# Layer-1 windowed attention: masks added on VectorE in the pass that takes a head's maximum, scores of the edge blocks as 512-column products

## The chip, the cores and the metric

The kernel runs on one core of one Trainium2 chip. The metric is the device time of one execution in microseconds; the time of a kernel is the median of its runs. TensorE (PE; its weight loads are shown apart as PEld) multiplies, VectorE (DVE) and ScalarE (ACT) work on what it leaves in PSUM, GpSimd (POOL) and the DMA queues work on SBUF only.

## What is computed

The reference is a trunk of two layers over 512 latent tokens with 256 context tokens in front. Layer 0 mixes with an mLSTM, layer 1 with windowed attention, and each layer ends in a squared-ReLU MLP. The change touches the attention of layer 1, cut here to what matters:

```python
# 16 query heads in 4 groups, one key/value head per group, head size 64, blocks of 128 queries
def block(args):                         # one of 4 query blocks
    j, qb = args
    kb = lax.dynamic_slice_in_dim(kp, j * SWA_BLOCK, 3 * SWA_BLOCK, axis=1)   # previous, own, next key block
    valid = (jnp.abs(rel) <= WINDOW) & (kpos >= 0) & (kpos < n_tok)           # WINDOW = 128
    s_lat = jnp.einsum("bqhgd,bkhd->bhgqk", qb, kb).astype(F32) * scale
    s_lat = jnp.where(valid, s_lat, -jnp.inf)
    s_ctx = jnp.einsum("bqhgd,bchd->bhgqc", qb, ck).astype(F32) * scale       # 256 context keys, no mask
    m = jnp.maximum(jnp.maximum(jnp.max(s_lat, -1), jnp.max(s_ctx, -1)), sink_g)
    p_lat, p_ctx = jnp.exp(s_lat - m[..., None]), jnp.exp(s_ctx - m[..., None])
    den = jnp.sum(p_lat, -1) + jnp.sum(p_ctx, -1) + jnp.exp(sink_g - m)
    o = jnp.einsum("bhgqk,bkhd->bqhgd", p_lat, vb) + jnp.einsum("bhgqc,bchd->bqhgd", p_ctx, cv)
    return o / jnp.moveaxis(den, 3, 1)[..., None]
```

A middle query block (j = 1, 2) sees three key blocks and the context, 640 keys; its previous block needs a triangular mask and its next block the opposite one. An edge block (j = 0, 3) sees two key blocks and the context, 512 keys, and needs one of the masks.

## The kernel before

**Scores** (`scores`, lines 1903 to 1958) makes the scores of one group g and one block j, head by head; it is a generator that yields after each of the four heads. Queries `qs` are the stationary operand, 128 tokens of one head with the high and low halves of the float split stacked, and the keys `ks` (two versions, `k0` and `k1`) are moved past them, so that each score is the sum of two products. A head of a middle block fills 640 columns of a PSUM tile `s` of its own; two heads of an edge block share one tile of 1024 columns, 512 each (`per = 2`). A tile is two PSUM banks, and the pool `sc` holds two tiles. For each head TensorE does, in order:

- L1925, L1926: two products of 256 columns against the context keys (`cx`),
- L1927: a product of 384 or 256 columns against the keys of the window (`lat`),
- L1929 and L1931: the masks. A mask `msk` of 128 × 128 in bf16, with 0 or a large negative number, is added to the first and to the last 128 columns of `lat` by a product with the identity `idb`; an edge block has only one of the two,
- L1932: the second product of the window.

Then VectorE takes the maximum of the tile (L1938 `mx`, for both heads of an edge pair at once), and makes from it and the sink the negative bias `nb` (L1940). ScalarE takes the exponential from PSUM into `e` and sums it into `den` (L1945). After every second head come the sink's exponential `es` (L1950, L1952), the denominator (L1953, L1954), and on GpSimd the division of `e` (L1956).

**Weigh** (`weigh`, from line 1960) turns the four heads' `e` by transposes on TensorE (L1972, into a tile `pt`), copies them by ScalarE to `ph` (L1977), and multiplies them with the values (L1989, L1995, tile `av`); VectorE adds the two halves into `yT` (L2000).

**The order** comes from `layer1_mix`. It steps through the 16 pairs of group and block, and a string written by hand, `PAT`, says for each what comes next: a head's scores (S), a turn of transposes (T), a step of the value products (V) or a step of filler work (F). Five heads are made ahead. The filler is work of other steps with matmuls of its own: values and queries of layer 1 (`pv`, `pq`, with rotary embedding on VectorE, ScalarE and GpSimd), and the output projection of the group before (`mm<-y`), whose sums VectorE adds to the residual `hL` (L1838). The framework adds the waits: an instruction that writes a tile waits for those that still read it. Instructions on one engine then run in the order shown, and a waiting one holds all behind it.

Of the kernel before, what the change touches and what calls it, by code (L numbers as in the profile page):

```python
# [9 lines left out]
F32 = mybir.dt.float32  # L10
F32R = mybir.dt.float32r
BF16 = mybir.dt.bfloat16
AF = mybir.ActivationFunctionType
ALU = mybir.AluOpType
AX = mybir.AxisListType
# [6 lines left out]
P = 128  # L22
D = 1024
KT = D // P
NL = 512
NCX = 256
T = NL + NCX
# [7 lines left out]
DH = 64  # L35
EPS = 1e-6
NEG = -1e30
# [19 lines left out]
class Trunk:  # L57
# [828 lines left out]
    def core(self, p, qkv):  # L886
# [46 lines left out]
        def weights(g, d, hh):  # L933
# [8 lines left out]
            for i in range(3):  # L942
# [5 lines left out]
        C = mc.tile([P, 5, 2, VW], F32, name="C", tag="C")  # L948
        seqs = ([4, 5, 0, 1, 2, 3], [5, 4, 3, 2, 1, 0])
        between = [[lambda: scores(0), lambda: weights(0, 0, 0)],  # L950
                   [lambda d=d, hh=hh: weights(0, d, hh) for d, hh in ((0, 1), (1, 0), (1, 1))]]
        for part, todo in zip((range(3), range(3, 5)), between):
# [21 lines left out]
        for g in range(2):  # L974
            if g:
                scores(1)
                if p < 3:
                    self.new_es(p + 1)
                for d in range(2):
                    for hh in range(2):  # L980
                        weights(1, d, hh)
                        yield 2
# [660 lines left out]
    def layer1_mix(self, u):  # L1643
        nc, tc, a = self.nc, self.tc, self.a
        self.ctx_ada.close()
        with tc.tile_pool(name="sw", bufs=1, reuse_waits="tile") as sw:
# [4 lines left out]
            nsink = sw.tile([P, HS], F32, name="nsink")  # L1651
            nc.gpsimd.tensor_scalar(out=nsink, in0=self.sink, scalar1=-1.0, scalar2=1.0, op0=ALU.mult, op1=ALU.mult)

            idb = sw.tile([P, P], BF16, name="idb")
            nc.gpsimd.tensor_copy(out=idb, in_=self.ident)
            msk = []
            for i, sgn in enumerate((1, -1)):
                mk = sw.tile([P, P], BF16, name=f"msk{i}")
                nc.gpsimd.memset(mk, 0.0)
                nc.gpsimd.affine_select(out=mk, in_=mk, compare_op=ALU.is_ge, fill=NEG, base=0, pattern=[[sgn, P]],  # L1660
                                        channel_multiplier=-sgn)
                msk.append(mk)
            ks = sw.tile([P, 2, KVH, T], F32R, name="ks")
            vst = [self.base.tile([P, 2, 2, DH], F32, name=f"vst{j}", tag=f"hC{j}") for j in range(NCH)]
            qs = {}
            self.swd = dict(ks=ks, vst=vst, qs=qs, nsink=nsink, idb=idb, msk=msk)

            rows = self.rows_of(u)
            for m in range(2):
# [233 lines left out]
    def scores(self, sw, g, j, scp, out):  # L1903

        nc = self.nc
        d = self.swd
        mm = nc.tensor.matmul
        q4 = d["qs"][g][:, :, j * P:(j + 1) * P]
        k0, k1 = [d["ks"][:, i, g, :] for i in range(2)]
        lo, hi = max(0, j - 1), min(4, j + 2)  # L1910
        wl = (hi - lo) * P
        W = wl + NCX
        den = sw.tile([P, 4], F32, name="den", tag="den", bufs=2)
        nb = sw.tile([P, 4], F32, name="nb", tag="nb", bufs=2)
        es = sw.tile([P, 4], F32, name="es", tag="es", bufs=2)
        per = 2 if W == 512 else 1
        views = []
        for i in range(4):
            if i % per == 0:
                s = scp.tile([P, 1024], F32, name="s", tag="s")  # L1920
                views = []
            ql = q4[:, i, :]
            c0 = (i % per) * 512 if per == 2 else 512 - wl
            lat, cx = s[:, c0:c0 + wl], s[:, c0 + wl:c0 + W]
            mm(out=cx, lhsT=ql, rhs=k0[:, NL:T], start=True, stop=False)  # L1925
            mm(out=cx, lhsT=ql, rhs=k1[:, NL:T], start=False, stop=True)  # L1926
            mm(out=lat, lhsT=ql, rhs=k0[:, lo * P:hi * P], start=True, stop=False)  # L1927
            if j > 0:
                mm(out=lat[:, 0:P], lhsT=d["idb"], rhs=d["msk"][0], start=False, stop=False)  # L1929
            if j < 3:  # L1930
                mm(out=lat[:, wl - P:wl], lhsT=d["idb"], rhs=d["msk"][1], start=False, stop=False)  # L1931
            mm(out=lat, lhsT=ql, rhs=k1[:, lo * P:hi * P], start=False, stop=True)  # L1932
            views.append(s[:, c0:c0 + W])
            if i % per == per - 1:
                i0 = i + 1 - per
                mx = sw.tile([P, 2], F32, name="mx", tag="mx", bufs=4)[:, 0:per]
                keep = self.tc.keep_in_program_order if g + j == 0 else lambda x: x
                keep(nc.vector.reduce_max(out=mx, in_=s.rearrange("p (h w) -> p h w", h=2) if per == 2 else views[0],  # L1938
                                          axis=AX.X))
                keep(nc.vector.scalar_tensor_tensor(  # L1940
                    out=nb[:, i0:i0 + per], in0=mx, scalar=-(DH ** -0.5),
                    in1=d["nsink"][:, g * 4 + i0:g * 4 + i0 + per], op0=ALU.mult, op1=ALU.min))
                for ii, sv in zip(range(i0, i0 + per), views):
                    e = sw.tile([P, 640], F32, name="e", tag="e", bufs=10)
                    nc.scalar.activation(out=e[:, :W], in_=sv, func=AF.Exp, scale=DH ** -0.5, bias=nb[:, ii:ii + 1],  # L1945
                                         accum_out=den[:, ii:ii + 1])
                    out.append(e)
            if i % 2:
                pr = slice(i - 1, i + 1)
                nc.vector.tensor_tensor(out=es[:, pr], in0=nb[:, pr],  # L1950
                                        in1=self.sink[:, g * 4 + i - 1:g * 4 + i + 1], op=ALU.add)
                nc.scalar.activation(out=es[:, pr], in_=es[:, pr], func=AF.Exp)  # L1952
                nc.vector.tensor_tensor(out=den[:, pr], in0=den[:, pr], in1=es[:, pr], op=ALU.add)  # L1953
                nc.vector.reciprocal(out=den[:, pr], in_=den[:, pr])  # L1954
                for ii in (i - 1, i):
                    nc.gpsimd.tensor_scalar(out=out[ii][:, :W], in0=out[ii][:, :W], scalar1=den[:, ii:ii + 1],  # L1956
                                            scalar2=1.0, op0=ALU.mult, op1=ALU.mult)
            yield
# [194 lines left out]
```

## Time and profile before

| | before |
|---|---|
| three runs | 1503.93, 1503.08, 1502.97 us |
| median | 1503.08 us |
| the profiled execution | 1502.54 us |
| its span | 1500.4 us, granted TensorE clock 0.996 |
| layer-1 attention in it | from about 950 to 1137 us |

The profile is one execution. Each row of a timeline gives the start, the duration, the engine, the line of the code, the operation, and the tiles that it writes and reads. Durations of matmuls overlap, because they are pipelined; the time from one start to the next says what one costs. A row of groups ends with the number of instructions, their busy time in us and the mean in ns, then the engine's idle time before them and what ended it. A row of waits names the engine that waited, its line and tile, what it waited for, and the sum in us, the number and the longest.

### The profile page before, as it was taken

To read this page: it belongs to the slowest core of one execution; us is meant where nothing else is said; L and a number is where in the kernel's file an instruction comes from. 1 tells how busy PE (TensorE), PEld (TensorE's weight loads), DVE (VectorE), ACT (ScalarE), POOL (GpSimd) and SP (SyncE) were. 2 spreads that over 40 slices of the span, in tenths; PEclk is the share of its full clock that TensorE was granted. 3 is DMA by queue.
4 is the path that set the end of the run, shared out by engine and by line. 5 is a ranking of instruction groups with operands and counts; after the bars stand their busy time and mean duration, and the time that the engine had idled before them with its cause. 6 is when DMAs were issued, how large, how long until landed. Compare 5 with 4: busy or idle time off the path is not lost.

```text
span 1500.4 us, 23047 instructions
## 1 busy us (share of the span) xinstructions
PE 1482.1 (99%) x8793; PEld 1309.1 (87%) x8793; DVE 1110.2 (74%) x1996; ACT 717.4 (48%) x1428; POOL 268.5 (18%) x263
## 2 busy tenths in 40 slices
PE   9999999999999999999999999999999999999998
PEld 5888888988889999999999998776767988888886
DVE  4886638497797878777787667767777874867697
ACT  4544343443674242423424244766676755545454
POOL 0112111212203222312223221133333000000000
PEclk9999999999999999999999999999999999999999
DMA  9223323144121334243442422311100533240211
GB/s 372 85 85 125 115 71 124 67 139 163 57 99 71 124 130 150 103 149 131 142 151 102 143 83 82 121 59 57 36 29 31 195 113 112 82 143 29 99 71 57
DMA packets 49317, 161.16 MB, mean 107 GB/s; under 512 B 5775, under 2 KB 8591, under 8 KB 49079
## 3 DMA queue, kind: packets, MB, share of 16 engines
q1 hardware_dynamic: 48032, 157.92, 30.6%
q10 hardware_dynamic: 1175, 1.77, 0.3%
q8 instruction: 69, 1.13, 0.3%
q14 instruction: 41, 0.34, 0.1%
HBM read 153.90 MB, written 2.10 MB: 104 GB/s over the span
## 4 chain that ended last, share of the span: by engine, by line
PE 91%; DVE 4%; ACT 2%; issue 1%; DMA 1%; POOL 1%; SPq 0%; POOLq 0%; DVEq 0%; ACTq 0%
PE mm L102 57%; PE p L102 10%; PE kept L102 3%; PE pt L1972 2%; PE pb L102 2%; PE pc L102 2%; PE pq L102 2%; PE av L1989 2%; PE acc L102 1%; PE at L1001 1%; PE s L1932 1%; PE arow L102 1%; PE at L958 1%; PE pk L102 1%; PE at L994 1%
## 5 line engine op out<-in xcount | busy, mean ns | idle before, releaser
L102 PE MATMUL mm<-h,whi 128*128 128x384 f32 x1024 | 262.5, 337 | 0.0
L1046 DVE TENSOR_TENSOR wlo<-raw,whi 128x1024 fp32r<-128x1024 f32 (+2 forms) x152 | 182.0, 1201 | 91.7 <-ACT whi L1045 89.3
L1045 ACT CAST whi<-raw 128x1024 fp32r<-128x1024 f32 (+2 forms) x152 | 151.0, 998 | 164.9 <-PE mm L102 106.9
L102 PE MATMUL mm<-uH,whi 128*128 128x512 f32 (+1 forms) x496 | 189.3, 386 | 0.0
L102 PE MATMUL mm<-uH,wlo 128*128 128x512 f32 (+1 forms) x496 | 186.7, 377 | 0.0
L102 PE MATMUL mm<-uL,whi 128*128 128x512 f32 (+1 forms) x496 | 186.2, 377 | 0.0
L102 PEld LDWEIGHTS mm<-h,whi 128*128 128x128 f32 x1024 | 185.4, 188 | 0.3 <-DVE h L1046 0.2
L269 DVE SCALAR_TENSOR_TENSOR adap<-raw,crow 128x1024 bf16<-128x1024 f32 x128 | 164.4, 1284 | 10.4 <-DMA raw<-ada 9.6
L102 PE MATMUL mm<-h,wlo 128*128 128x384 f32 x512 | 172.1, 336 | 0.0
L102 PE MATMUL p<-t,whi 128*128 128x384 f32 x448 | 114.2, 336 | 0.0
L1045 ACT CAST whi<-sum 128x512 fp32r<-128x512 f32 (+1 forms) x42 | 31.8, 760 | 161.6 <-PE mm L102 83.4
L102 PEld LDWEIGHTS mm<-uH,wlo 128*128 128x128 f32 x496 | 93.4, 188 | 17.5 <-issue 0.2
L102 PEld LDWEIGHTS mm<-uL,whi 128*128 128x128 f32 x496 | 93.6, 189 | 15.4 <-DVE uL L1091 0.3
L102 PEld LDWEIGHTS mm<-uH,whi 128*128 128x128 f32 x496 | 93.0, 189 | 15.2 <-issue 0.2
L102 PEld LDWEIGHTS mm<-h,wlo 128*128 128x128 f32 x512 | 96.1, 188 | 0.0
L1046 DVE TENSOR_TENSOR wlo<-wb,whi 128x1024 fp32r<-128x1024 f32 x49 | 59.1, 1219 | 36.2 <-ACT whi L1045 36.1
L1046 DVE TENSOR_TENSOR h<-r,h 128x384 fp32r<-128x384 f32 (+2 forms) x100 | 58.1, 583 | 31.3 <-ACT h L1045 30.9
L102 PEld LDWEIGHTS p<-t,whi 128*128 128x128 f32 x448 | 81.3, 188 | 0.0
L1045 ACT CAST whi<-wb 128x1024 fp32r<-128x1024 f32 x49 | 51.6, 1053 | 57.5 <-PE mm L102 47.9
L1956 POOL TENSOR_SCALAR e<-e,den 128x512 f32<-128x512 f32 (+1 forms) x64 | 53.7, 852 | 139.2 <-DVE den L1954 74.2
L102 PE MATMUL mm<-uC,whi 128*128 128x256 f32 x416 | 78.2, 287 | 0.3 <-ACT whi L1045 0.3
L102 PE MATMUL p<-t,wlo 128*128 128x384 f32 x224 | 75.3, 336 | 0.0
(423 smaller groups left out, 3509.7 us busy)
## 6 DMA issues: line engine op xcount, KB each, us to landing
raw<-ada SPq DMA_DIRECT2D x80, 512.0 KB, 3.3
raw<-w SPq DMA_DIRECT2D x64, 512.0 KB, 3.3
raw<-w2a SPq DMA_DIRECT2D x32, 512.0 KB, 3.2
wb<-w2b SPq DMA_DIRECT2D x28, 512.0 KB, 3.5
adaw<-ada SPq DMA_DIRECT2D x16, 512.0 KB, 11.3
raw<-wqk SPq DMA_DIRECT2D x8, 512.0 KB, 4.3
raw<-wv SPq DMA_DIRECT2D x8, 512.0 KB, 3.2
raw<-wo SPq DMA_DIRECT2D x8, 512.0 KB, 3.3
```

What stands on the lines that cost most here:

```text
L102: i = self.nc.tensor.matmul(**kw)
L269: self.tc.keep_in_program_order(nc.vector.scalar_tensor_tensor(out=pr, in0=w, scalar=0.5, in1=self.crow[:, v, :], op0=ALU.mult, op1=ALU.mu ...
L958: mm(out=kv[d][64 * h:64 * h + 64, n * VW:(n + 1) * VW], lhsT=kp[:, d, j, 64 * h:64 * h + 64], rhs=v[:, j, h, :], start=True, stop=True)
L994: mm(out=os[d][hh][:, ob], lhsT=qs[d][HP[hh], j * P:(j + 1) * P], rhs=C[HP[hh], n - 1, d, :], start=not started, stop=False)
L1001: mm(out=o[hh][:, i * VW:(i + 1) * VW], lhsT=pw[g, d, hh][:, i, :], rhs=v[:, 3 * g + i, hh, :], start=False, stop=i == 2)
L1045: keep(self.nc.scalar.copy(out=hi, in_=src))
L1046: keep((eng or self.nc.vector).tensor_tensor(out=lo, in0=src, in1=hi.bitcast(F32), op=ALU.subtract))
L1932: mm(out=lat, lhsT=ql, rhs=k1[:, lo * P:hi * P], start=False, stop=True)
L1956: nc.gpsimd.tensor_scalar(out=out[ii][:, :W], in0=out[ii][:, :W], scalar1=den[:, ii:ii + 1], scalar2=1.0, op0=ALU.mult, op1=ALU.mult)
L1972: nc.tensor.transpose(out=pt[:, i * P:(i + 1) * P], in_=ps_[i][:, n * P:(n + 1) * P], identity=self.ident)
L1989: mm(out=o[i * DH:(i + 1) * DH, :], lhsT=v(n + i), rhs=pq[n + i], start=n == 0, stop=n == len(blks) - 2)
```

## The change

There are no products with masks any more. A tile `msk` of 768 columns holds zeros with the two triangles in place, and views of it fit each kind of block. For each head one instruction of VectorE, `tensor_tensor_reduce`, adds the mask to the scores in place in PSUM and takes the maximum of the sum; `nb` is made per head instead of per pair. A middle head now has four products (256, 256, 384, 384 columns). An edge head has two of 512 columns, which hold the window and the context together: in block 3 these columns lie together in `ks`, in block 0 they are two runs of 256 with a gap, which the product reads in one access pattern. The tiles, their pool and `PAT` stay as they are.

```diff
-            idb = sw.tile([P, P], BF16, name="idb")
-            nc.gpsimd.tensor_copy(out=idb, in_=self.ident)
-            msk = []
-            for i, sgn in enumerate((1, -1)):
-                mk = sw.tile([P, P], BF16, name=f"msk{i}")
-                nc.gpsimd.memset(mk, 0.0)
...
+            wide = sw.tile([P, 6 * P], BF16, name="msk")
+            msk, edge = wide[:, :5 * P], wide.rearrange("p (c t) -> p c t", c=2)[:, :, :NCX]
+            nc.gpsimd.memset(wide, 0.0)
+            for c0, sgn in ((0, 1), (2 * P, -1)):
+                nc.gpsimd.affine_select(out=msk[:, c0:c0 + P], in_=msk[:, c0:c0 + P], compare_op=ALU.is_ge, fill=NEG,
+                                        base=0, pattern=[[sgn, P]], channel_multiplier=-sgn)
+            msk = {0: msk[:, P:], 1: msk, 2: msk, 3: edge}
...
-            lat, cx = s[:, c0:c0 + wl], s[:, c0 + wl:c0 + W]
-            mm(out=cx, lhsT=ql, rhs=k0[:, NL:T], start=True, stop=False)
-            mm(out=cx, lhsT=ql, rhs=k1[:, NL:T], start=False, stop=True)
-            mm(out=lat, lhsT=ql, rhs=k0[:, lo * P:hi * P], start=True, stop=False)
-            if j > 0:
-                mm(out=lat[:, 0:P], lhsT=d["idb"], rhs=d["msk"][0], start=False, stop=False)
-            if j < 3:
-                mm(out=lat[:, wl - P:wl], lhsT=d["idb"], rhs=d["msk"][1], start=False, stop=False)
-            mm(out=lat, lhsT=ql, rhs=k1[:, lo * P:hi * P], start=False, stop=True)
-            views.append(s[:, c0:c0 + W])
-            if i % per == per - 1:
...
-                keep(nc.vector.reduce_max(out=mx, in_=s.rearrange("p (h w) -> p h w", h=2) if per == 2 else views[0],
-                                          axis=AX.X))
...
+            sv = s[:, c0:c0 + W]
+            if per == 2:
+                def cols(t):
+                    return t.rearrange("p (c t) -> p c t", t=NCX)[:, 0::2] if j == 0 else t[:, lo * P:T]
+                o = sv.rearrange("p (c t) -> p c t", t=NCX) if j == 0 else sv
+                mm(out=o, lhsT=ql, rhs=cols(k0), start=True, stop=False)
+                mm(out=o, lhsT=ql, rhs=cols(k1), start=False, stop=True)
+            else:
+                for o, cs in ((s[:, 512:512 + NCX], slice(NL, T)), (s[:, c0:512], slice(lo * P, hi * P))):
+                    mm(out=o, lhsT=ql, rhs=k0[:, cs], start=True, stop=False)
+                    mm(out=o, lhsT=ql, rhs=k1[:, cs], start=False, stop=True)
+            mx = sw.tile([P, 1], F32, name="mx", tag="mx", bufs=4)
...
+            mv = sv.rearrange("p (c t) -> p c t", t=NCX) if j == 3 else sv
+            keep(nc.vector.tensor_tensor_reduce(out=mv, in0=mv, in1=d["msk"][j], scale=1.0, scalar=-3e38,
+                                                op0=ALU.add, op1=ALU.max, accum_out=mx))
+            keep(nc.vector.scalar_tensor_tensor(
+                out=nb[:, i:i + 1], in0=mx, scalar=-(DH ** -0.5),
+                in1=d["nsink"][:, g * 4 + i:g * 4 + i + 1], op0=ALU.mult, op1=ALU.min))
```

How the change moves instructions shows in the order of each engine. First TensorE in group 2, block 0, from the value products of the block before to the second head of the first edge pair. Before the change (`s_10893` is the tile of the pair, `av_10900` that of the values, `mm_10929` a projection):

```order
L1989 MATMUL av_10900<-ph_10811,vst1_9544 64x512
L1989 MATMUL av_10900<-ph_10818,vst2_9545 64x512
L1989 MATMUL av_10900<-ph_10845,vst3_9546 64x512
L1989 MATMUL av_10900<-ph_10873,vst4_9547 64x512 [waits Activation_49]
L1995 MATMUL av_10900<-ph_10885,vst5_9548 64x256 [waits Activation_49]
L1995 MATMUL av_10900<-ph_10885,vst5_9548 64x256
L1925 MATMUL s_10893<-ks_9542,qs_10388 128x256
L1926 MATMUL s_10893<-ks_9542,qs_10388 128x256
L1927 MATMUL s_10893<-ks_9542,qs_10388 128x256
L1931 LDWEIGHTS idb_9530
L1931 MATMUL s_10893<-msk1_9537,idb_9530 128x128
L1932 MATMUL s_10893<-ks_9542,qs_10388 128x256
```

The second head's products wait for nothing, and a mask stands among them. The same place after the change (`s_10833` is the tile of the pair; its first row is the last product of the first head):

```order
L1926 MATMUL s_10833<-ks_9538,qs_10353 128x512 [waits DMAHW7_49,DMAHW1_49,DMAHW0_49]
L1984 MATMUL av_10842<-ph_10754,vst1_9540 64x512
L1984 MATMUL av_10842<-ph_10761,vst2_9541 64x512
L1984 MATMUL av_10842<-ph_10790,vst3_9542 64x512
L1984 MATMUL av_10842<-ph_10813,vst4_9543 64x512
L1990 MATMUL av_10842<-ph_10825,vst5_9544 64x256 [waits Activation_49]
L1990 MATMUL av_10842<-ph_10825,vst5_9544 64x256
L102 MATMUL mm_10866<-y000_10603,whi_10777 128x512 [waits DVE_49]
L1925 MATMUL s_10833<-ks_9538,qs_10353 128x512 [waits Activation_49]
L1926 MATMUL s_10833<-ks_9538,qs_10353 128x512
```

The second head has two wide products, one projection product has moved ahead of it, and it waits for ScalarE: for the exponential of the first head, which reads the same tile. Second, VectorE at the same pair, before:

```order
L1938 TENSOR_REDUCE mx_10916<-s_10893 128x2 [waits PE_49]
L2000 TENSOR_TENSOR yT1_10483<-av_10900,yb_10907 64x2x128 [waits Activation_49]
L2000 TENSOR_TENSOR yT1_10483<-av_10900,yb_10907 64x2x128
L1940 SCALAR_TENSOR_TENSOR nb_10891<-mx_10916,nsink_9528 128x2 [waits DVE_49]
L1950 TENSOR_TENSOR es_10892<-nb_10891,sm_67 128x2 [waits DVE_49]
```

And after (`ISA` is the new pass and, in the row behind it, the reading of its maximum):

```order
L1934 ISA s_10833,mx_10836<-s_10833,msk_9530 128x512 [waits PE_49]
L1934 ISA mx_10836 128x1
L1949 RECIPROCAL den_10709<-den_10709 128x2 [waits DVE_49]
L1936 SCALAR_TENSOR_TENSOR nb_10831<-mx_10836,nsink_9528 128x1 [waits DVE_49]
L1995 TENSOR_TENSOR yT1_10443<-av_10842,yb_10849 64x2x128 [waits Activation_49]
L1995 TENSOR_TENSOR yT1_10443<-av_10842,yb_10849 64x2x128
L1934 ISA s_10833,mx_10855<-s_10833,msk_9530 128x512 [waits PE_49]
L1934 ISA mx_10855 128x1
L1936 SCALAR_TENSOR_TENSOR nb_10831<-mx_10855,nsink_9528 128x1 [waits DVE_49]
L1945 TENSOR_TENSOR es_10832<-nb_10831,sm_67 128x2 [waits DVE_49]
```

One reduction and one bias for the pair have become two passes, two reads and two biases, and the sum `yT` of the block before stands between the two heads instead of behind the reduction.

More of the change, by code (lines that the diff above doesn't have):

```diff
@@ L1652, in layer1_mix @@
             nc.gpsimd.tensor_scalar(out=nsink, in0=self.sink, scalar1=-1.0, scalar2=1.0, op0=ALU.mult, op1=ALU.mult)
-            idb = sw.tile([P, P], BF16, name="idb")
-            nc.gpsimd.tensor_copy(out=idb, in_=self.ident)
-            msk = []
-            for i, sgn in enumerate((1, -1)):
-                mk = sw.tile([P, P], BF16, name=f"msk{i}")
-                nc.gpsimd.memset(mk, 0.0)
-                nc.gpsimd.affine_select(out=mk, in_=mk, compare_op=ALU.is_ge, fill=NEG, base=0, pattern=[[sgn, P]],
-                                        channel_multiplier=-sgn)
-                msk.append(mk)
+            wide = sw.tile([P, 6 * P], BF16, name="msk")
[5 more added lines that the diff above has]
+            msk = {0: msk[:, P:], 1: msk, 2: msk, 3: edge}
             ks = sw.tile([P, 2, KVH, T], F32R, name="ks")
@@ L1665, in layer1_mix @@
             qs = {}
-            self.swd = dict(ks=ks, vst=vst, qs=qs, nsink=nsink, idb=idb, msk=msk)
+            self.swd = dict(ks=ks, vst=vst, qs=qs, nsink=nsink, msk=msk)
             rows = self.rows_of(u)
@@ L1916, in scores @@
         per = 2 if W == 512 else 1
-        views = []
         for i in range(4):
@@ L1920, in scores @@
                 s = scp.tile([P, 1024], F32, name="s", tag="s")
-                views = []
             ql = q4[:, i, :]
             c0 = (i % per) * 512 if per == 2 else 512 - wl
-            lat, cx = s[:, c0:c0 + wl], s[:, c0 + wl:c0 + W]
-            mm(out=cx, lhsT=ql, rhs=k0[:, NL:T], start=True, stop=False)
-            mm(out=cx, lhsT=ql, rhs=k1[:, NL:T], start=False, stop=True)
-            mm(out=lat, lhsT=ql, rhs=k0[:, lo * P:hi * P], start=True, stop=False)
-            if j > 0:
-                mm(out=lat[:, 0:P], lhsT=d["idb"], rhs=d["msk"][0], start=False, stop=False)
@@ L1930, in scores @@
-            if j < 3:
-                mm(out=lat[:, wl - P:wl], lhsT=d["idb"], rhs=d["msk"][1], start=False, stop=False)
-            mm(out=lat, lhsT=ql, rhs=k1[:, lo * P:hi * P], start=False, stop=True)
-            views.append(s[:, c0:c0 + W])
-            if i % per == per - 1:
[L1935 to L1938, printed above, removed]
-                                          axis=AX.X))
[L1940 to L1947, printed above, removed]
@@ new lines, in scores @@
+            mx = sw.tile([P, 1], F32, name="mx", tag="mx", bufs=4)
+            keep = self.tc.keep_in_program_order if g + j == 0 else lambda x: x
+            mv = sv.rearrange("p (c t) -> p c t", t=NCX) if j == 3 else sv
[4 more added lines that the diff above has]
+                in1=d["nsink"][:, g * 4 + i:g * 4 + i + 1], op0=ALU.mult, op1=ALU.min))
@@ L1948, in scores @@
+            e = sw.tile([P, 640], F32, name="e", tag="e", bufs=10)
+            nc.scalar.activation(out=e[:, :W], in_=sv, func=AF.Exp, scale=DH ** -0.5, bias=nb[:, i:i + 1],
+                                 accum_out=den[:, i:i + 1])
+            out.append(e)
             if i % 2:
```

## The prediction

> **What bounds the kernel now.** I read the page first: its busy line and the chain that ended last.
>
> ```profile
> span 1500.4 us, 23047 instructions
> PE 1482.1 (99%) x8793; PEld 1309.1 (87%) x8793; DVE 1110.2 (74%) x1996; ACT 717.4 (48%) x1428; POOL 268.5 (18%) x263
> PE 91%; DVE 4%; ACT 2%; issue 1%; DMA 1%; POOL 1%; SPq 0%; POOLq 0%; DVEq 0%; ACTq 0%
> ```
>
> TensorE has work in 99% of the span and carries 91% of the chain. So removed matmul time is gain only as long as nothing makes TensorE wait instead. The edit touches layer-1 attention alone: by the timeline its first score product starts at about 950 us and its last value product ends at about 1137. The view of windows cuts this stretch (columns: window, its length, then busy us and instruction counts of PE, PEld, DVE, ACT, POOL, then clock and DMA).
>
> ```profile
> 950.00:1137.00 187.00, 183.11 (x1102) 133.94 (x1102) 137.57 (x300) 128.00 (x291) 60.70 (x70) 1.00 0.17 53
> 950.00:970.00 20.00, 18.60 (x125) 15.63 (x126) 16.43 (x35) 13.54 (x32) 4.32 (x6) 1.00 0.37 120
> 970.00:1008.00 38.00, 38.00 (x227) 28.36 (x226) 25.97 (x52) 25.54 (x57) 14.44 (x15) 1.00 0.22 63
> 1008.00:1046.00 38.00, 35.51 (x203) 24.81 (x202) 29.89 (x63) 26.40 (x58) 12.80 (x14) 1.00 0.15 46
> 1046.00:1137.00 91.00, 91.00 (x553) 65.14 (x550) 65.28 (x152) 62.52 (x147) 29.13 (x37) 1.00 0.11 37
> ```
>
> For 129 of the 187 us (970 to 1008, 1046 to 1137) TensorE has no gap at all, at full granted clock. Its gaps lie in the first block and from 1008 to 1046. VectorE has 137.57 us of work in 187: 74%. TensorE is the bound, VectorE has room on average, and what counts is when each of its results comes.
>
> **Matmul time removed.** The timeline of TensorE over one head of a middle block, and over one head of an edge block (first or last):
>
> ```profile
> 1062.81 0.28 PE L1925 MATMUL s<-ks,qs 128*128 128x256 f32 x1
> 1062.92 0.28 PE L1926 MATMUL s<-ks,qs 128*128 128x256 f32 x1
> 1063.04 0.33 PE L1927 MATMUL s<-ks,qs 128*128 128x384 f32 x1
> 1063.22 0.23 PE L1929 MATMUL s<-msk,idb 128*128 128x128 bf16 x1
> 1063.57 0.40 PE L102 MATMUL pq<-uH,whi 128*128 128x512 f32 x1
> ...
> 1052.94 0.39 PE L102 MATMUL mm<-y,wlo 128*128 128x512 f32 x1
> 1053.17 0.28 PE L1925 MATMUL s<-ks,qs 128*128 128x256 f32 x1
> 1053.77 0.62 PE L102 MATMUL mm<-y,whi 128*128 128x512 f32 x2
> ```
>
> Durations overlap, so I price from start to start. A middle head takes 1063.57 − 1062.81 = 0.76 us. Of that 256 columns cost 0.115 each and 384 cost 0.18, so without masks it takes 2 × 0.115 + 2 × 0.18 = 0.59: 0.17 saved. An edge head takes 1053.77 − 1053.17 = 0.60; a 512-column product takes 1053.17 − 1052.94 = 0.23, two take 0.46: 0.14 saved. With 32 heads of each kind: 5.4 + 4.5 = **9.9 us** off TensorE. The first block's edge product reads its columns in two runs of 256, which no row of before shows. Its bounds are 0.23 and two 256-column products' 2 × 0.115 = 0.23, so I count no difference.
>
> **VectorE's new pass.** The masked sum and maximum, in place in PSUM, is shown by no row. The nearest ones, from the groups by form and from the views of two source lines:
>
> ```profile
> L1938 DVE TENSOR_REDUCE mx<-s 128x1 f32<-128x640 f32 x32 | 26.3, 821 | 6.7 <-PE s L1932 6.2
> L1938 DVE TENSOR_REDUCE mx<-s 128x2 f32<-128x1024 f32 x16 | 19.4, 1215 | 4.6 <-PE s L1932 4.5
> L1940 DVE SCALAR_TENSOR_TENSOR nb<-mx,nsink 128x1 f32<-128x1 f32 x32 | 5.5, 172 | 0.4
> L1838 DVE SCALAR_TENSOR_TENSOR hL<-mm,mod,hL 128x512 f32<-128x512 f32 x22 | 16.4, 747 | 5.0 <-PE mm L102 4.7
> L269 DVE SCALAR_TENSOR_TENSOR adap<-raw,crow x128: 1194/1218/2305, 103.1 to 846.3; 128x1024 bf16<-128x1024 f32 x128
> L269 DVE DVE_READ_ACCUMULATOR adap<-raw,crow x128: 74/81/86, 104.3 to 847.5; 128x1 f32 x128
> ```
>
> An operation with two inputs and an accumulator ran 1024 elements in 1.218 us, then 0.081 for reading the accumulator; one with a PSUM input ran 512 in 0.747. The low bound for 512 is half the reduction's 1.215 (0.61), the high bound is twice per element (1.2). I take 0.72 for 512 and 0.85 for 640, nearest to L269 and L1838, plus 0.08 for the accumulator. An edge head then costs 0.72 + 0.08 + 0.17 = 0.97 where half a pair cost (1.215 + 0.19) / 2 = 0.70; a middle head costs 0.93 where it cost 0.82. Added: 32 × 0.27 + 32 × 0.11 = 12 us. VectorE goes to about 150 of 177 us, 85%. No bound by itself, but queues get longer.
>
> [...]
>
> **The new wait.** Before, both heads of an edge pair were multiplied into one tile, and one reduction followed. Now the first head's pass and exponential touch the tile before the second head's product is issued, and by the order that product waits for the first head's exponential (ScalarE). Queued behind it on TensorE is everything else: value products, projections, transposes. The length of that chain, from a stretch of the timeline:
>
> ```profile
> 966.03 0.42 PE L1932 MATMUL s<-ks,qs 128*128 128x384 f32 x1
> 966.49 0.82 DVE L1938 TENSOR_REDUCE mx<-s 128x1 f32<-128x640 f32 x1 [0.27 <-PE s L1932]
> 967.35 0.16 DVE L1940 SCALAR_TENSOR_TENSOR nb<-mx,nsink 128x1 f32<-128x1 f32 x1
> 967.61 0.80 ACT L1945 ACTIVATE e<-s,nb 128x640 f32<-128x640 f32 x1
> 968.54 0.39 PE L1925 MATMUL s<-ks,qs 128*128 128x256 f32 x1
> ```
>
> Here every step was served at once: 968.54 − 966.03 = 2.51 us from the last product's start to the next product on the tile. TensorE itself is through with that last product after 0.26, which leaves 2.25. For 512 columns the exponential is 0.11 shorter (0.69 against 0.80 in the row below) and the pass with its accumulator 0.02: 2.12. So a second head with less than 2.12 us of TensorE work between the halves waits even when both engines are idle.
>
> ```profile
> L1945 ACT ACTIVATE e<-s,nb 128x512 f32<-128x512 f32 x32 | 21.8, 688 | 5.2 <-DVE nb L1940 5.2
> ```
>
> What stands between the halves is priced from start to start as above; value products and transposes by these rows of TensorE's timeline:
>
> ```profile
> 1061.15 0.69 PE L1972 MATMUL pt<-ident,e 128*128 128x128 f32 x4
> 1061.59 0.48 PE L102 MATMUL pq<-uH,whi 128*128 128x512 f32 x1
> ...
> 1091.65 1.94 PE L1989 MATMUL av<-ph,vst 128*64 128x512 f32 x8
> 1093.42 0.60 PE L1995 MATMUL av<-ph,vst 128*64 128x256 f32 x4
> 1093.95 0.38 PE L1925 MATMUL s<-ks,qs 128*128 128x256 f32 x1
> ```
>
> In group 2, block 0, the order has a middle block's value products there, 1093.95 − 1091.65 = 2.30 us, and one projection product of 0.23: 2.5. Four transposes take 0.44. Added up like this, in the 14 pairs behind the first block the work between the halves is 3.7, 3.1, 3.7, 1.8, 3.6, 2.3, 2.5, 2.5, 2.8, 2.5, 2.5, 2.5, 3.6 and 2.3 us. With free engines only the 1.8 waits: 0.3 in all. But VectorE is 85% busy, and its order has the residual addition (0.747, L1838) or the output additions between such steps. With one such operation in front the chain is 2.87, and nine pairs wait: 1.07 + 2 × 0.57 + 5 × 0.37 + 0.07 = **4.1 us**. With two it is 3.62, and ten wait: 1.8 + 2 × 1.3 + 5 × 1.1 + 0.8 + 0.5 = 11.2 us. I take the middle one, since a queue of one suits a load of 85%, and keep 0.3 and 11.2 as ends. Three middle heads come close behind an edge head in the same way (2.6, 2.6 and 2.75 us): +0.7.
>
> **The first block.** There the order has 1.8, 0.5, 1.2 and 2.1 us between a head and the product that waits for it, since little other work is ready. At a chain of 2.12 that is 0.3 + 1.6 + 0.9 + 0 = 2.8, and 0.4 for one more operation of a VectorE that is 82% busy there: 3.2. What goes is TensorE's wait for the rotated queries, because more projection products now stand before that point. The waits of before in the window:
>
> ```profile
> PE s L1925 <- DVE qs L1888: 1.0, 1, 1.0
> PEld s L1925 <- ACT e L1945: 3.2, 5, 1.1
> PEld pt L1972 <- POOL e L1956: 4.7, 10, 1.2
> ```
>
> So + 3.2 − 1.0 = **+2.2 us**. The POOL waits stay: transposes stand 5 us or more behind their last head in both orders, except in that first block.
>
> **Edits at no cost.** On GpSimd one copy and two fills of 128 columns give way to a fill of 768, far ahead of the first use; the 16 more small operations for the bias are in VectorE's sum. The exponentials and all DMAs but the mask's are unchanged.
>
> **Sum.** −9.9 + 4.1 + 0.7 + 2.2 = −2.9 us. The profiled execution took 1502.54 us (1500.4 of it span), so it would take 1499.6. It lies 0.5 under the median of the three runs, 1503.08, so the forecast for a median is about **1500.2 us**. A measurement of this kernel can tell about 0.2%, 3 us; faster means under 1500.1, slower over 1506.1.
>
> **Rivals.**
> 1. *The waits are hidden.* Each late product lets VectorE and ScalarE catch up, so the next chain runs at 2.12 us: pairs 0.3, first block 2.8 − 1.0 = 1.8, others 0. Then −9.9 + 2.1 = −7.8: **1494.7**, as a median 1495.3. For it: two stretches of 38 and 91 us without one gap, although 3.2 us of waits for exponentials turn up in the weight-load rows. [...] Chance 0.27.
> 2. *The edge pairs become the bound.* Two operations stand before each step of the chain: −9.9 + 11.2 + 0.7 + 2.2 = +4.2: **1506.7**, as a median 1507.3. It is slower on balance from 7.0 us of pair waits, half a microsecond in each of 14. For it: VectorE's share, and the bias operation, which now comes per head. Against it: TensorE's own waits give the queues time. Chance 0.18.
> 3. *The new pass is dear.* At 1.2 us for 512 and 1.5 for 640 VectorE would have 150 + 32 × 0.48 + 32 × 0.65 = 186 us of work for a window of 177 to 187: with a twentieth idle it sets 196, so + 9: **1512**. The gain is gone from about 0.95 us for 512. Against it: no two-input row runs at such a rate. Chance 0.05.
> 4. *The wide products aren't what they seem.* In the first block of each group a product's moving columns come in two runs with a gap. If that cost a second pass, 16 heads × 2 products × 0.23 = 7.4 us would be added: −2.9 + 7.4 = +4.5, **1507**. Against it: two separate products of 256 columns need only 2 × 0.115. Chance 0.05.
>
> **How the numbers follow.** The forecast's own case, 1497 to 1504, has 0.45; rivals 1 to 4 have 0.27, 0.18, 0.05 and 0.05. Somewhat under half of the forecast's case, 0.18, lies below 1500.1 and 0.27 above. Faster: 0.27 + 0.18 = 0.45. Slower, rivals 2 to 4: 0.18 + 0.05 + 0.05 = 0.28. The same: 0.27. The range takes in the first two rivals and leaves out the third and the edges of the others: 1494 to 1508.
>
> **What would show it.** Right: score products in start-to-start steps of 0.23 for 512 columns, no mask rows, about 173 us of TensorE work in the window; rows of the new pass near 0.72 and 0.85 us with a read of 0.08; and in the waits a large row of score products for the exponential, 7 to 9 us where it was 3.2. Wrong: that row at 3 or below (rival 1), or above 12 (rival 2), a pass above 0.95 (rival 3), or first-block products with 0.4 us from start to start (rival 4). If new waits stand at transposes or value products instead, the step from pairs to time is wrong even if the time fits.

## The result, and the profile after

The changed kernel took 1507.26 us (median of 6 runs, 1506.53 to 1509.51), the kernel before 1502.13 us in 6 runs beside it: a ratio of 1.0035, 95% interval 1.0025 to 1.0045. It is slower by about 5 us, where 1500.2 and a small gain were forecast. The page of the profiled execution (span, busy line, chain):

```profile
span 1505.1 us, 22832 instructions
PE 1478.8 (98%) x8632; PEld 1299.5 (86%) x8633; DVE 1114.8 (74%) x2092; ACT 718.3 (48%) x1428; POOL 270.2 (18%) x261
PE 87%; DVE 7%; ACT 3%; issue 2%; POOL 1%; DMA 0%; SPq 0%; POOLq 0%; DVEq 0%; ACTq 0%
```

TensorE is busy 3 us less in a span 5 us longer, and 4% of the chain has gone from it, mostly to VectorE and ScalarE. By the timelines the stretch from the start of the first score product to the start of the last value product grew from 195.5 to 201.6 us, 6.1 more; from there to the end both kernels take 354.8. Ahead of the stretch the changed kernel is 1.5 us shorter in these two executions. The granted clock was 0.50 there for 3.4 us (from 37.0 us), and for 6.8 us (from 35.6 us) in the trace of before; by estimate the difference, 3.4 us at half the clock, is worth up to 1.7 us (a product of 512 columns took 0.43 us there to the next start, 38.08 to 38.51 us of before, where it takes 0.23 at a clock of 1.00). So the loss arose in the attention. (The stretch ends at 1145.6 us in the trace of before, not at about 1137 as the prediction had it; the three rows of waits that its sum uses are the same up to 1152 us.)

The new pass, in the groups by form of the changed kernel:

```profile
L1934 DVE CUSTOM_DVE_ANT_0 s<-s,msk 128x640 f32<-128x640 f32 x32 | 26.5, 829 | 5.6 <-PE s L1930 5.4
L1934 DVE CUSTOM_DVE_ANT_0 s<-s,msk 128x512 f32<-128x512 f32 x16 | 11.1, 696 | 6.2 <-PE s L1926 3.5 <-PE pt L1967 1.8 <-ACT whi L1045 0.8
L1934 DVE CUSTOM_DVE_ANT_1 s<-s,msk 128x512 f32<-128x512 f32 x16 | 11.1, 692 | 6.1 <-PE pt L1967 3.2 <-PE s L1926 1.9 <-ACT y L1811 0.9
L1934 DVE DVE_READ_ACCUMULATOR2_ANT mx<- 128x1 f32 x64 | 8.6, 134 | 0.2
L1936 DVE SCALAR_TENSOR_TENSOR nb<-mx,nsink 128x1 f32<-128x1 f32 x64 | 13.2, 206 | 1.1
```

These rows add up to 70.5 us; what they replace, by the prediction's rows and `nb` for pairs (3.0), was 54.2: 16 us more of VectorE's instructions. The pass itself is as cheap as assumed, the read of its maximum dearer (0.13 us for 0.08). But the durations of VectorE's small instructions overlap those of their neighbours, so its busy time grew by much less. The windows of the whole stretch, before and after:

```profile
950.18:1145.64 195.46, 191.75 (x1153) 140.25 (x1153) 141.89 (x307) 132.26 (x298) 62.01 (x71) 1.00 0.16 51
948.67:1150.24 201.57, 189.79 (x992) 131.59 (x993) 147.99 (x403) 133.48 (x298) 63.76 (x71) 0.99 0.16 50
```

VectorE is busy 6.1 us more, and 73% of the stretch in both. The prediction added the sum of durations, 12 us, to a busy time and came to 85%. The waits in the changed kernel:

```profile
PEld pt L1967 <- POOL e L1951: 8.6, 16, 1.1
PEld s L1929 <- ACT e L1940: 4.8, 6, 1.8
PEld s L1925 <- ACT e L1940: 4.7, 10, 1.2
PE pt L1967 <- POOL e L1951: 3.8, 9, 0.8
PE s L1929 <- ACT e L1940: 3.0, 4, 1.4
PE s L1925 <- ACT e L1940: 1.4, 3, 0.7
PE s L1925 <- DVE qs L1886: 0.9, 1, 0.9
```

Score products' waits for exponentials went from 3.2 to 9.5 us at the weight loads (4.8 and 4.7), and transposes' waits for GpSimd from 4.7 to 8.6. One pair of group 2, block 0 in the timeline (weight loads and GpSimd left out) shows how a second head comes to wait:

```profile
1084.71 0.40 PE L1926 MATMUL s<-ks,qs 128*128 128x512 f32 x1
...
1084.99 1.17 DVE L1886 TENSOR_TENSOR qs<-rt,qs 64x512 fp32r<-64x512 f32 x1
...
1086.28 0.69 DVE L1934 CUSTOM_DVE_ANT_1 s<-s,msk 128x512 f32<-128x512 f32 x1
...
1086.96 0.74 DVE L1836 SCALAR_TENSOR_TENSOR hL<-mm,mod,hL 128x512 f32<-128x512 f32 x1
...
1087.69 0.15 DVE L1936 SCALAR_TENSOR_TENSOR nb<-mx,nsink 128x1 f32<-128x1 f32 x1
...
1087.95 0.69 ACT L1940 ACTIVATE e<-s,nb 128x512 f32<-128x512 f32 x1 [0.58 <-DVE nb L1936]
...
1088.79 0.50 PE L1925 MATMUL s<-ks,qs 128*128 128x512 f32 x1 [0.72 <-ACT e L1940]
1089.12 0.40 PE L1926 MATMUL s<-ks,qs 128*128 128x512 f32 x1
1089.36 0.40 PE L102 MATMUL mm<-y,wlo 128*128 128x512 f32 x1
```

A rotary addition stands in front of the pass, and a residual addition between the pass and its bias: 4.08 us from product to product, with 0.72 us of idle TensorE. The product that has waited also takes 0.33 us to the next start (1088.79 to 1089.12), where a first score product behind a projection that hasn't waited takes 0.23. That is no general price of waiting: behind value products or transposes the first score product mostly takes 0.31 to 0.34 us in e1 too, with no idle time before it.

The table sets the runs side by side by the start-to-start times of all matmuls in the stretch. The lower quartile for the same kind, size and neighbours over all runs counts as work; what lies more than 0.05 us above it counts as waiting, put down to the product that came late (us, one execution of each kernel, good to some 2 us):

| kernel | ratio to before, 95% interval | stretch | work | waiting: scores | transposes | others |
|---|---|---|---|---|---|---|
| before | 1 | 195.5 | 187.6 | 3.0 | 4.8 | 0.1 |
| changed | 1.0035, 1.0025 to 1.0045 | 201.6 | 180.7 | 10.2 | 9.3 | 1.5 |
| e1 pair products first | 0.9966, 0.9954 to 0.9979 | 192.8 | 178.7 | 3.5 | 8.8 | 1.7 |
| e2 masks left out | 0.9954, 0.9941 to 0.9968 | 189.4 | 178.7 | 2.6 | 6.3 | 1.8 |
| e3 middle blocks only | 0.9974, 0.9963 to 0.9985 | 191.6 | 183.0 | 3.1 | 5.0 | 0.7 |
| e4 edge blocks only | 1.0046, 1.0033 to 1.0058 | 203.4 | 184.0 | 8.7 | 10.6 | 0.2 |
| e5 first block only | 1.0012, 1.0003 to 1.0021 | 197.6 | 180.7 | 8.3 | 7.2 | 1.4 |
| e6 own tile | 0.9981, 0.9972 to 0.9989 | 192.7 | 179.9 | 3.7 | 7.1 | 2.1 |
| e7 more VectorE work | 1.0037, 1.0024 to 1.0049 | 200.9 | 178.7 | 6.8 | 13.0 | 2.3 |
| e8 one bias per pair | 0.9982, 0.9973 to 0.9991 | 192.5 | 180.1 | 4.0 | 7.1 | 1.3 |
| e9 the same, later | 1.0028, 1.0016 to 1.0039 | 200.5 | 178.7 | 6.6 | 12.9 | 2.3 |
| e10 e1 with lead six | 0.9969, 0.9958 to 0.9981 | 191.1 | 182.3 | 2.4 | 4.8 | 1.6 |
| e11 before with lead six | 0.9986, 0.9977 to 0.9995 | 194.1 | 190.4 | 2.7 | 0.5 | 0.6 |
| e12 VectorE work spread | 1.0036, 1.0023 to 1.0050 | 203.6 | 181.3 | 3.8 | 15.8 | 2.8 |

Lost clock stands under waiting, not under work: e7 has the work of e1 although its clock was 0.50 for 10.2 us of the stretch. The five executions of e1 all ran at a mean clock of 0.998, those of the other kernels at 0.992 to 0.999, and the ratios contain that difference; the stretch leaves out what the clock did elsewhere.

### The profile page after: what moved, and what is told of

Read it like the earlier page. It is cut to its first block, busy times and chain, and to the rows that moved or that the text cites. A ratio compares the mean times of both kernels' runs of the same rounds, so it can differ in the third digit from the quotient of the medians.

```text
span 1505.1 us, 22832 instructions
## 1 busy us (share of the span) xinstructions
PE 1478.8 (98%) x8632; PEld 1299.5 (86%) x8633; DVE 1114.8 (74%) x2092; ACT 718.3 (48%) x1428; POOL 270.2 (18%) x261
## 4 chain that ended last, share of the span: by engine, by line
PE 87%; DVE 7%; ACT 3%; issue 2%; POOL 1%; DMA 0%; SPq 0%; POOLq 0%; DVEq 0%; ACTq 0%
PE mm L102 55%; PE p L102 10%; PE kept L102 3%; PE pb L102 2%; PE pc L102 2%; PE pq L102 2%; PE pt L1967 1%; PE acc L102 1%; PE at L1001 1%; PE av L1984 1%; POOL e L1951 1%; DVE wlo L1046 1%; ACT e L1940 1%; PE at L958 1%; PE arow L102 1%
## 5 line engine op out<-in xcount | busy, mean ns | idle before, releaser
L269 DVE SCALAR_TENSOR_TENSOR adap<-raw,crow 128x1024 bf16<-128x1024 f32 x128 | 164.0, 1281 | 11.3 <-DMA raw<-ada 10.6
## 6 DMA issues: line engine op xcount, KB each, us to landing
adaw<-ada SPq DMA_DIRECT2D x16, 512.0 KB, 11.2
```

What stands on the lines that cost most here:

```text
L269: self.tc.keep_in_program_order(nc.vector.scalar_tensor_tensor(out=pr, in0=w, scalar=0.5, in1=self.crow[:, v, :], op0=ALU.mult, op1=ALU.mu ...
```

## The experiments

Theory W: the loss comes from the second head of an edge pair, which waits for the exponential of the first in its tile. Rival V: it comes from VectorE's added work, which makes every head late. Rival S: the matmul saving isn't there.

**e1, pair products first.** Both heads of an edge pair are multiplied before the first pass; VectorE's work stays.

```diff
+            views[i] = sv
+            if per == 2 and i % 2 == 0:
+                yield
+                continue
+            for n in range(i + 1 - per, i + 1):
...
```

> The changed kernel, but in the edge blocks both heads of a pair are multiplied before the first of the two VectorE passes is issued, so that no product waits for an exponential that reads the other half of its tile; VectorE's work is the same. If the pair waits carry the loss (theory W), TensorE's stalls at score products fall from 10 to about 5 us and the time to 1498 to 1502 us. If VectorE's longer work carries it (rival V), the transposes and score products wait for the same late results as before and the time stays at 1505 to 1508. If the matmul saving isn't there (rival S), the time comes out at 1503 to 1506 with short waits.

Measured 1498.18 us, a ratio of 0.9966: faster than the kernel before by 5 us and than the changed one by 10. W's forecast held, V's didn't. Its waits:

```profile
PEld pt L1973 <- POOL e L1957: 8.0, 20, 0.7
PEld s L1930 <- ACT e L1946: 4.1, 9, 1.5
PE s L1930 <- ACT e L1946: 0.7, 1, 0.7
```

The wait for exponentials at the weight loads, 4.1 us, is near the 3.2 of before; that of the transposes, 8.0, has stayed.

**e2, masks left out.** The kernel before without mask products, with wide edge products and the old maximum.

```diff
-            if j > 0:
-                mm(out=lat[:, 0:P], lhsT=d["idb"], rhs=d["msk"][0], start=False, stop=False)
-            if j < 3:
-                mm(out=lat[:, wl - P:wl], lhsT=d["idb"], rhs=d["msk"][1], start=False, stop=False)
```

> The kernel before with all masks left out of the computation (its output lacks them) and the edge scores as 512-column products; the maximum is taken per pair as before. Only TensorE's share of the change is left. W and V both expect the whole saving of matmul time, 7 to 10 us less than before: 1492 to 1495. S expects less than 4 us: 1498 or more.

Measured 1496.72 us, 0.9954: 6.9 us less by the ratio, just under the 7 to 10 that W and V expect, and against S. TensorE's work fell by 187.6 − 178.7 = 8.9 us, but its waits rose by 2.8, so the stretch is only 6.1 shorter. Its transposes wait for GpSimd 7.1 us where it was 4.7, with nothing added to VectorE and no product held by its neighbour's exponential:

```profile
PEld pt L1975 <- POOL e L1959: 7.1, 14, 1.1
```

With 8.9 us less to do TensorE met GpSimd sooner here. What VectorE's new passes and biases cost when no tile holds anything up is the difference to e1: 192.8 − 189.4 = 3.4 us of the stretch (0.0012 of the ratio, 1.8 us, with overlapping intervals).

**e3 and e4, half of the change each.** Middle blocks in the new way and edge blocks in the old, and the other way round:

```diff
+    def scores(self, sw, g, j, scp, out):
+        return (self.scores_new if j in (1, 2) else self.scores_old)(sw, g, j, scp, out)   # e4: j in (0, 3)
```

> The new pass in the middle blocks alone; edge blocks as before, with masks by TensorE and one maximum for a pair. No product waits for an exponential on its own tile. W expects about half of the matmul saving, 4 to 5 us less than before: 1497 to 1499. V expects the 32 middle heads' share of VectorE's added work, about 5 of 16 us, to take most of it: 1500 to 1503.

> The new pass in the edge blocks alone; middle blocks as before. All 16 waits of second heads are there, and about 11 of the 16 us that VectorE gets to do. W expects the whole loss and half the saving, 1508 to 1512. V expects a part of the loss, 1503 to 1507.

Measured 1499.25 us (0.9974) and 1510.71 us (1.0046). The middle blocks bring a gain of 3.9 us by the ratio, close to W's 4 to 5 and outside V's range; the edge blocks alone lose 7, more than the whole change, as W has it. The loss sits in the edge blocks.

**e5, the first block only.** The rule of e1 in group 0, block 0 alone (`both = per == 2 and g + j == 0`).

> The changed kernel, with both products of a pair ahead of the passes in the very first block alone; the 14 later pairs keep their wait. In the trace of the changed kernel the first block has 6.1 us of stalls against 1.7 before, and 3 us at a granted clock of 0.50 behind them. If the waits add up by place, this kernel gains the 4 to 6 us of the first block and comes to 1501 to 1504, the later pairs keeping 3 to 5 us of loss. If the first block's loss is only shifted (VectorE then is late elsewhere), it stays at 1505 or more.

Measured 1503.61 us, 1.0012: 0.0023 of the ratio, 3.5 us, came from the first block, and 0.0046, 7 us, from the 14 later pairs. By the stretches it is 201.6 − 197.6 = 4.0 us and 197.6 − 192.8 = 4.8 us; part of the 7 may be e1's even clock. The waits add up by place. What the first block looks like in the changed kernel, by windows (PE, PEld, DVE, ACT, POOL busy, then the granted clock):

```profile
964.00:966.00 2.00, 1.03 (x5) 0.36 (x3) 1.50 (x6) 1.51 (x2) 0.00 (x0) 1.00 0.00 0
966.00:968.00 2.00, 0.86 (x5) 0.54 (x4) 1.67 (x7) 1.47 (x4) 0.00 (x0) 1.00 0.26 66
968.00:970.00 2.00, 1.37 (x6) 0.85 (x7) 1.53 (x6) 1.26 (x5) 1.06 (x2) 0.71 0.52 127
970.00:972.00 2.00, 2.00 (x10) 1.83 (x9) 1.34 (x6) 1.14 (x3) 1.43 (x2) 0.50 0.52 205
972.00:974.00 2.00, 2.00 (x10) 0.93 (x9) 1.51 (x4) 1.79 (x5) 0.92 (x3) 0.94 0.00 0
```

TensorE is busy 1.9 us of 4, and then its clock is halved for some 3.4 us (0.58, 1 and 0.12 of three windows). In this place the traces of before, e1, e2, e3 and e5 show no such drop, that of e4 does. The 3.5 us hold both the idle time and the clock, 0.50 for 3.4 us, which by estimate costs at most 1.7; no run separates them.

**e6, a tile for each edge head.** The passes stay one by one, but no two heads share a tile (`per = 1` throughout).

> The changed kernel, with a tile of its own for every edge head, so that a product waits for the exponential of two heads before, not for that of the neighbour in its tile. If the shared tile is the cause, this cures most of it: 1499 to 1503. If VectorE's work or the order of passes were the cause, nothing changes: 1505 to 1509. It could also be worse, since two tiles then hold two heads instead of four: over 1509.

Measured 1500.26 us, 0.9981. The waits at scores fall to 3.7 us. So it is the shared tile and not the order of the passes that makes the wait. Whether e1 is faster than this can't be told: the intervals overlap, and the stretch is the same (192.7 and 192.8 us).

**e7 and e9, more work on VectorE.** e1 with 32 further maxima that nobody uses; e9 leaves those of the first block out.

```diff
             if i % 2:
+                junk = sw.tile([P, 1], F32, name="junk", tag="junk", bufs=2)
+                nc.vector.reduce_max(out=junk, in_=self.cs, axis=AX.X)
```

> The kernel with pair products first, and one more maximum of 512 columns of a resident table on VectorE for every second head (32 in all, about 0.6 us each, 19 us), whose result nobody uses. It is more than the 16 us that the change adds to VectorE. If VectorE's work is what costs (rival V), the time goes up by 5 us or more over the 1498.2 of the kernel without it, to 1503 or above. If only the waits of second heads cost (theory W), by 0 to 3 us.

> As the run with more work on VectorE, but without it in the first block (30 of the 32 extra maxima are left, 18 us). That run was 0.7% slower than the kernel with pair products first, 10.7 us, and its granted clock was 0.50 from about 966 to 977 us, in and behind the first block. If the clock and the first block carry most of this, 30 extra maxima cost 2 to 5 us: 1500 to 1503. If VectorE's load costs wherever it lies, 7 us or more: 1505 or above.

Measured 1509.0 us (1.0037) and 1507.29 us (1.0028). Both lie in V's range, but the experiment went wrong: the table `cs` is ready early, and the scheduler moved the maxima forward. In e9 all 30 ran between 931 and 993 us, ten of them in the first block:

```profile
950.00:972.00 22.00, 16.52 (x94) 13.33 (x93) 21.78 (x46) 12.10 (x26) 2.32 (x2) 0.99 0.50 152
```

VectorE is busy 21.78 of 22 us there, TensorE 16.52, and the clock fell to 0.50, for 10.2 us from 966.2 in e7 and for 6.8 from 971.3 in e9; that alone is by estimate worth up to 5.1 and 3.4 us. What the two runs price is VectorE's work in and near the first block, where it has no room, and the clock.

**e8, one bias for a pair.** e1 with `nb` made once for an edge pair.

> The kernel with pair products first and, as before the change, one bias operation for a pair: 16 fewer VectorE operations of 0.2 us, but the first exponential waits for the second pass too. If VectorE's operations delay the transposes, 1 to 2 us less than 1498.2; if the later first exponential matters as much, the same within 1 us.

Measured 1500.01 us, 0.9982. Its interval overlaps that of e1. There is no gain from 16 fewer small operations: the transposes' waits for GpSimd at the weight loads fell from 8.0 to 6.8 us, but the score products' waits for exponentials rose from 4.1 to 6.8.

**e10 and e11, six heads ahead.** `for _ in range(6)` where five heads are made before the first block is weighed, in e1 and in the kernel before.

> The kernel with pair products first, and six heads instead of five multiplied ahead of the weighing, so that heads come earlier in front of their transposes. If the transposes wait because heads come late in a chain over VectorE, ScalarE and GpSimd, their waits for GpSimd (8.0 us at weight loads) fall to 5 or less and the time by 1 to 3 us, to 1495 to 1497. If GpSimd or VectorE sets a pace of its own, nothing moves: 1497.5 to 1499.

> The kernel before with six heads ahead: the control for the run above. With TensorE busy 98% of the stretch, there is little to gain: 0 to 1.5 us less, 1501 to 1503. If more lead helps both alike, it is no property of the change.

Measured 1498.83 us (0.9969) and 1500.56 us (0.9986). In e10 the transposes' waits for GpSimd fell from 8.0 to 4.1 us at the weight loads, as expected, but the median did not follow. The profiled execution did: 1496.89 us where that of e1 took 1498.35, and a stretch 1.7 us shorter. The other five took 1497.78 to 1499.46 at clocks of 0.995 to 0.997, where e1 had 0.998; they left no traces. My expectation for the median failed, and why isn't settled. The kernel before gains 2 us from the longer lead, a little more than expected.

**e12, VectorE work spread over the later blocks.**

```diff
+            for r in ([0, 1] if per == 2 and i == 3 else [i - 2] if per == 1 and i >= 2 else []) if g + j else []:
+                junk = sw.tile([P, 1], F32, name="junk", tag="junk", bufs=2)
+                nc.vector.reduce_max(out=junk, in_=out[r][:, :W], axis=AX.X)
```

> In the two runs with more work on VectorE the extra maxima read a table that is ready early, and by the trace nearly all of them ran before or in the first block, where VectorE had no room (21.8 us busy of 22). Here the kernel with pair products first gets 30 extra maxima that each read a head's exponential after GpSimd's division, outside the first block, so that they spread over the other 15 blocks: 30 at 0.6 to 0.8 us, about 21 us, which nobody waits for. If VectorE's work as such costs (rival V), 5 us or more over the kernel without it, a ratio to the kernel before of 1.000 or above. If only its place in the first block cost, 0 to 3 us: 0.9965 to 0.9985.

Measured 1508.67 us, 1.0036: 0.0070 of the ratio, 10.5 us, over e1, as V has it. The groups by form and the waits:

```profile
L1951 DVE TENSOR_REDUCE junk<-e 128x1 f32<-128x640 f32 x16 | 12.8, 817 | 2.2 <-POOL e L1960 2.1
L1951 DVE TENSOR_REDUCE junk<-e 128x1 f32<-128x512 f32 x14 | 9.5, 683 | 1.3 <-POOL e L1960 1.1
```

```profile
PEld pt L1976 <- POOL e L1960: 15.8, 25, 1.9
PE pt L1976 <- POOL e L1960: 7.8, 13, 1.5
PEld s L1930 <- ACT e L1946: 4.3, 10, 0.9
DVE junk L1951 <- POOL e L1960: 3.3, 5, 1.1
```

22.3 us of work that nobody waits for, with VectorE busy 162.7 us of the stretch instead of e1's 146.8, doubled the transposes' waits at the weight loads (8.0 to 15.8) and left those of the score products alone. The maxima brought waits of their own into VectorE's queue (3.3 us), and the clock was 0.50 twice for 3.4 us, by estimate worth up to 3.4 us, so this isn't load alone. It is also 16 us of busy time, where the change itself added 6. V is right that VectorE's time is not free here, and wrong about where most of the loss came from: VectorE's work is the same in e1, which wins.

## Why the prediction was wrong

**Right.** TensorE is the bound (busy in 98% of the changed kernel's span, 87% of its chain), and what its waits do decides. The pass in PSUM took 0.69 and 0.83 us where 0.72 and 0.85 were assumed; rival 3 falls. Its 1.2 us for 512 columns and 1.5 for 640 were the author's estimate, twice the reduction's time per element, and no run shows a pass that takes so long: the longest in the changed kernel took 0.87. Wide products in two runs cost 0.23 us like the others, and a middle head lost its masks' time: rival 4 falls. Score products' waits for exponentials were forecast at 7 to 9 us and came to 9.5. The three terms for score products, 4.1 + 0.7 + 2.2 = 7.0 us, met 10.2 − 3.0 = 7.2, but that is partly luck, as the parts show.

**Wrong in its parts.** The later pairs' own idle time is smaller than 4.1: nine of them waited 3.4 us in all (0.89 the longest). One middle head alone waited 1.4 us (at 1025.02), where 0.7 was put down for three. The first block is dearer than 2.2: the count of waiting there went from 2.5 to 7.9 us, and e5 gives 4.0 for it. The step "what goes is TensorE's wait for the rotated queries" failed: that wait is 0.9 us where it was 1.0. And behind 1.9 us of work in 4 the clock was 0.50 for 3.4 us, which no term had. The choice of a queue of one rested on a VectorE that is 85% busy; it is 73% busy.

**The steps that failed.** The stretches of e2, e1 and e5 take the loss apart, one difference at a time (single executions, so good to a us or two):

| from, to | what is added | forecast | measured |
|---|---|---|---|
| before, e2 | no mask products, wide edge products | −9.9 | 189.4 − 195.5 = −6.1 |
| e2, e1 | VectorE's passes and biases | 0 | 192.8 − 189.4 = +3.4 |
| e1, e5 | wait in the shared tile, 14 later pairs | +4.1 + 0.7 | 197.6 − 192.8 = +4.8 |
| e5, changed | the same in the first block | +2.2 | 201.6 − 197.6 = +4.0 |
| sum | | −2.9 | +6.1 |

First, "The POOL waits stay". The distance in the order, 5 us and more, was taken as enough, and the transposes' waits were put at nothing. They went from 4.8 to 9.3 us, with 1.4 more at other products. That new waits stand at transposes was the prediction's own sign of a wrong step from pairs to time. Most of that does not come from the waits in the tile: e1, without these, still has 8.8, and e2, where only TensorE's work is less, has 6.3. What e1 has more comes with VectorE's new work, which the sum put at no cost; e12 shows that more work on VectorE lengthens these waits further. Second, "9.9 us off TensorE" as a gain: e1 and e2 confirm 8.9 of work, of which e2 turned 6.1 into time. (That the changed kernel's work is 2.0 above e1's is within the table's error and stays open; the clock isn't the reason, since e5 without a drop has the same 180.7.) Third, the first block, put at 2.2 us, cost 4.0.

Rival 2 named the right side and the time, 1507.3, but not the way: it wanted 11.2 us of waits in the 14 later pairs, and e5 against e1 gives 4.8 by the stretch and 7 by the ratio for these pairs with all their consequences. That its number fits is luck.

The chance of a slower result, 0.28, was too low for what the order already showed: 16 new waits on a path through three engines, each of which could only add time, against a saving of TensorE's work that was known to 1 us.

## What to carry to other kernels

When a product is split from its partner in a shared tile, look in the order for the wait between them before counting the saving: here an operation that works in place on half a tile held the other half as well, and issuing both products first turned a loss of 5 us into a gain of 5. Work taken off the bound engine was not all gain: its next waits, those of the transposes, came nearer, and 8.9 us less work gave 6.1 us. Gaps on the bound engine that came close together went with a lower clock besides: in the changed kernel 0.50 for 3.4 us, behind 1.9 us of work in 4. And work put on an engine that is busy three quarters of the time was not free in any place that was tried, neither in and near the first block (e9) nor spread over the others (e12). Its load is to be read from busy time, since the durations of its small instructions overlap: here they added 16 us where the busy time grew by 6.1.

## What the runs showed of the hardware

In the changed kernel the granted clock fell to 0.50 without any long gap: TensorE had been busy 1.9 us of 4, with no idle stretch over 1.0 us. In e12 it fell to 0.50 twice, here behind 2.1 us of work in 4:

```profile
1086.00:1088.00 2.00, 1.41 (x7) 0.80 (x5) 1.78 (x8) 1.84 (x4) 0.48 (x1) 1.00 0.00 0
1088.00:1090.00 2.00, 0.68 (x3) 0.36 (x3) 2.00 (x5) 0.25 (x2) 2.00 (x2) 1.00 0.00 0
1090.00:1092.00 2.00, 1.89 (x10) 1.54 (x10) 0.72 (x5) 1.07 (x2) 0.06 (x1) 0.74 0.69 252
1092.00:1094.00 2.00, 2.00 (x10) 1.70 (x9) 0.87 (x3) 1.27 (x3) 0.00 (x0) 0.50 0.06 18
```

Within the attention the drop shows in the traces of the changed kernel, e4, e7, e9 and e12, the five that are slower than before by over 0.2%, and in no other. In the 3.4 us ahead of it TensorE was busy 0.55 to 1.95 us. That share alone doesn't decide: in e4 another 3.4 us with 1.56 us of work (1031.1 to 1034.5) brought no drop. The longest gap ahead of a drop was 2.4 us, in e9. What sets the drop off is not shown.

A bias of 128 × 1 usually takes 0.16 us. In the changed kernel five of 64 took 0.54 to 1.25 us, two of them in this stretch (timeline of VectorE and GpSimd):

```profile
1022.47 2.35 POOL L1951 TENSOR_SCALAR e<-e,den 128x640 f32<-128x640 f32 x2 [5.35 <-ACT ph L1972]
...
1023.38 0.67 DVE L1936 SCALAR_TENSOR_TENSOR nb<-mx,nsink 128x1 f32<-128x1 f32 x1
...
1024.79 1.76 POOL L1876 TENSOR_TENSOR rt<-rt,rx 128x512 f32<-128x512 f32 x1
1025.32 1.25 DVE L1936 SCALAR_TENSOR_TENSOR nb<-mx,nsink 128x1 f32<-128x1 f32 x1
```

Both ran while GpSimd was at work, and the longer one ended when GpSimd's addition did (1026.57 against 1026.55). The traces bear this out: of the 816 biases in all fourteen, 65 took over 0.4 us (3 of 48 in before, 5 of 64 in the changed kernel), and each of these ended within 0.02 us of the end of a GpSimd instruction; none that ran with GpSimd idle took over 0.17 us. So the long ones wait for GpSimd by all appearance, but no run changed GpSimd's work to test it. Such a bias stands in every head's chain.
